# A two-layer encoder on one core: other SBUF places for V's weights, ScalarE function tables loaded at set points, a new instruction order

## The chip, the core and the metric

The kernel runs on one core of one Trainium2 chip. A core has a matrix engine (PE; its weight loads are shown apart as PEld), two vector engines (DVE and POOL), a scalar engine (ACT) and a queue engine (SP) that here only issues DMA transfers. Each engine executes its own instructions strictly in the order in which the program holds them; between engines they wait on semaphores. The metric is the device time of one execution in microseconds, 1428.3 us before the change (median of 3 runs).

## The reference

One sequence of 512 tokens, width 1024, float32, passes through two layers; each has a token mixer and a SwiGLU channel mixer, both with an RMS norm ahead and one behind.

```python
def swiglu(x, w_gate, w_up, w_down):
    return (jax.nn.silu(x @ w_gate) * (x @ w_up)) @ w_down
...
    for layer in range(DEPTH):
        j = layer // N_MIXERS
        h = rms_norm(x, norm_mix_pre[layer])
        if layer % N_MIXERS == 0:
            h = neighbourhood_attention(h, na_w_qkv[j], na_w_o[j], na_rpb[j])
        else:
            h = dilated_attention(h, dil_w_qkv[j], dil_w_o[j])
        x = x + rms_norm(h, norm_mix_post[layer])
        h = rms_norm(x, norm_ffn_pre[layer])
        x = x + rms_norm(swiglu(h, ffn_w_gate[layer], ffn_w_up[layer], ffn_w_down[layer]), norm_ffn_post[layer])
```

Layer 0's mixer is a windowed attention over an 8 x 64 grid of tokens with a relative bias, 16 heads of 64. Layer 1's mixer is a mixture of three dilated sliding-window attentions, each with its own q, k and v (so nine projections of 1024 x 1024), merged by their softmax denominators. The hidden width of SwiGLU is 2816. The softmaxes need Exp, SwiGLU needs Silu.

## The kernel before

**Products.** Every large product is made of three float32r matmuls: each operand is split into a high part `h` (a copy by ACT, line 456) and a low part `l` (a subtraction by DVE, line 457), and `mm3` (lines 468 to 470) adds h x h, h x l and l x h in one PSUM bank. A matmul names a stationary operand, loaded 128 x 128 by PEld, and a moving operand that is streamed; here the stationary one changes with every matmul. The q/k projections (`pp_n`, `pp_d`), the gate and up projections (`gu`) and the v projections (`vn`, `vd`) are Strassen-Winograd products with seven products in place of eight: classes `Seven` and `Values`. In `Seven` (a "unit") the weights are stationary and the activations are streamed; in `Values` and in `v_quarter` (`vp_n`, `vp_d`), which together make V, the weights are streamed and the activations are stationary. Both kinds take 256 columns at a time. The steps of a unit are p1, p2, d1, s2, s4, s3 and x2b, twelve matmuls each; between them ACT and DVE move partial sums out of the bank (`sink`; line 946 is the subtraction between s3 and x2b in the gate and up projections, line 548 the copy between d1 and s4).

**Places.** Split weights go to four pairs of 4096-byte buffers (`wslot`), and where more are needed to parts of `vbig` and of `rxc`. In the built program `rxa`, `rxb` and `rxc`, which hold the split activations, begin at 128 modulo 512 bytes and the buffers of `wslot` at 448; `vbig` begins at 448 too, and its second half lies 536 columns behind the first, that is 96 bytes further modulo 512. The three pairs of buffers that V uses besides (`vslots`) begin at 224 and 448.

**Functions.** ACT holds the table of one set of functions at a time. Copy and Square are in each; the build puts an ACT_TABLE_LOAD ahead of the first Exp or Silu after the other one: lines 681, 948, 1347 and 948 again.

**Order.** The kernel is first recorded, as a list of some 14,700 instructions. `Order` then builds their dependences, runs a list scheduler 20 times forwards and backwards with the costs of `_cost`, takes the ranks of one of these runs (`FIRST`), changes some ranks by the rows of `TABLE`, and pins the order of each engine (`pin`). So a row of the table or a cost moves instructions on all engines. SP's and POOL's DMA issues are ordered so too.

**Stages, by the first and last start of their matmuls in the trace (us).** V of layer 0 from 9, its q/k projections and attention from 45 to 213, the output projection from 180 to 237, gate and up from 239 to 462, down from 460 to 566; V of layer 1 from 567 to 700, its q/k projections and attention from 689 to 1066, the output projection from 1013 to 1088, gate and up from 1090 to 1314, down from 1308 to 1415. Stages overlap where the order lets work of the next one fill gaps.

## Time and profile before

| | |
|---|---|
| runs | 1426.39, 1428.39, 1428.3 us; median 1428.3 |
| profiled execution, own time | 1425.52 us |
| its span | 1423.7 us |
| PE | 1393.9 us busy (98%), 10714 matmuls |
| PEld | 1302.8 us (92%) |
| DVE | 1186.0 us (83%) |
| ACT | 914.8 us (64%) |
| POOL | 534.9 us (38%) |
| DMA | 253.21 MB, mean 178 GB/s |

A matmul is pipelined: its record lasts about 0.28 us while the next begins about 0.115 us later, so that a busy PE says only that it is never empty. How fast it goes is seen from the starts: from how many matmuls fall into a stretch.

### The profile page before, as it was taken

Reading aid. Unit: us, or ns where it says so; the run is one execution under the profiler, and the core shown is the slowest. Engines: PE = TensorE matmul, PEld = TensorE weight load, DVE = VectorE, ACT = ScalarE, POOL = GpSimd, SP = SyncE. Lnnn points to the kernel's source line nnn. Section 1 sums busy time; section 2 is a strip of 40 time slices with the busy share of each in tenths; the row PEclk is TensorE's granted clock in tenths of the full one; section 3 lists DMA queues with packets and bytes.
Section 4 is the critical chain, followed back from the end, with each engine's and each line's share of the span. In section 5 each row is a group of like instructions: output and inputs, shape, how many; then the busy total and the mean of one; then the engine's idle time right before and its main releaser. Section 6 shows DMA issues by size and latency. Waiting matters only on the chain.

```text
span 1423.7 us, 27815 instructions
## 1 busy us (share of the span) xinstructions
PE 1393.9 (98%) x10714; PEld 1302.8 (92%) x10714; DVE 1186.0 (83%) x1891; ACT 914.8 (64%) x1850; POOL 534.9 (38%) x394
## 2 busy tenths in 40 slices
PE   8999999999999999999999999999999999999997
PEld 8998878999999888999999999998888999999886
DVE  7789868899998889997677788887658989988877
ACT  6488865654555667744477687887766555555664
POOL 3756525634320001666454344343215543430001
PEclk9999999999999999999999999999999999999999
DMA  7357598587334665545332353343776797845662
GB/s 254 125 179 192 163 314 240 202 237 214 119 110 137 221 216 173 173 156 179 134 113 75 113 172 98 99 142 98 252 222 216 219 258 219 255 145 164 207 215 96
DMA packets 86645, 253.21 MB, mean 178 GB/s; under 512 B 19312, under 2 KB 31600, under 8 KB 84464
## 3 DMA queue, kind: packets, MB, share of 16 engines
q1 hardware_dynamic: 77696, 197.69, 41.8%
q0 software_dynamic: 8672, 53.48, 15.0%
q8 instruction: 84, 1.38, 0.4%
q14 instruction: 49, 0.40, 0.1%
q10 hardware_dynamic: 144, 0.26, 0.0%
HBM read 229.24 MB, written 68.29 MB: 209 GB/s over the span
## 4 chain that ended last, share of the span: by engine, by line
PE 81%; DVE 9%; ACT 4%; DMA 2%; issue 2%; POOL 0%; POOLq 0%; DVEq 0%; SPq 0%; ACTq 0%
PE gu L468 8%; PE gu L469 8%; PE gu L470 8%; PE pp_d L468 5%; PE pp_d L469 4%; PE pp_d L470 4%; PE yd_s L469 3%; PE yd_s L468 3%; PE yd_s L470 3%; PE vd L469 2%; PE vd L470 2%; PE vd L468 2%; PE yd_pp L470 2%; PE yd_pp L469 2%; PE yd_pp L468 2%
## 5 line engine op out<-in xcount | busy, mean ns | idle before, releaser
L676 POOL TENSOR_TENSOR rs_yd<-v_yd,consts 128x1 f32<-128x1 f32 x8 | 10.0, 1256 | 251.9 <-DVE v_yd L674 251.9
L468 PE MATMUL gu<-rxa,h_c 128*128 128x256 f32 x352 | 98.6, 280 | 1.4 <-DVE mem L944 1.0
L469 PE MATMUL gu<-rxc,h_a 128*128 128x256 f32 x352 | 98.0, 279 | 1.0 <-DVE rxc L693 1.0
L468 PE MATMUL gu<-rxc,h_a 128*128 128x256 f32 x352 | 97.7, 278 | 0.5 <-ACT rxc L690 0.5
L469 PE MATMUL gu<-rxa,h_b 128*128 128x256 f32 x352 | 97.6, 277 | 0.2 <-DVE rxa L693 0.2
L470 PE MATMUL gu<-rxc,l_a 128*128 128x256 f32 x352 | 97.6, 278 | 0.0
L469 PE MATMUL gu<-rxa,h_c 128*128 128x256 f32 x352 | 97.3, 277 | 0.0
L470 PE MATMUL gu<-rxa,l_c 128*128 128x256 f32 x352 | 97.3, 277 | 0.0
L470 PE MATMUL gu<-rxa,l_b 128*128 128x256 f32 x352 | 97.3, 277 | 0.0
L456 ACT ACTIVATE rxc<-mem 128x512 fp32r<-128x512 f32 (+2 forms) x92 | 57.5, 633 | 61.8 <-PE yd_pp L469 32.9
L468 PE MATMUL gu<-rxa,h_b 128*128 128x256 f32 x352 | 97.1, 277 | 0.0
L457 DVE TENSOR_TENSOR rxc<-mem,rxc 128x512 fp32r<-128x512 f32 (+2 forms) x92 | 66.3, 730 | 18.9 <-ACT rxc L456 18.6
L536 POOL TENSOR_TENSOR r_d<-r_d 128x512 f32<-128x512 f32 x24 | 38.4, 1601 | 108.2 <-DVE l_ad L457 83.3
L536 POOL TENSOR_TENSOR raw<-raw 128x512 f32<-128x512 f32 x24 | 36.3, 1514 | 110.0 <-DVE l_a L457 109.9
L536 POOL TENSOR_TENSOR r_gu<-r_gu 128x512 f32<-128x512 f32 x20 | 29.6, 1480 | 116.8 <-DVE l_a L457 104.6
L468 PEld LDWEIGHTS gu<-rxa,h_c 128*128 128x128 f32 x352 | 66.1, 188 | 3.1 <-DVE mem L944 1.7
L469 PEld LDWEIGHTS gu<-rxc,h_a 128*128 128x128 f32 x352 | 66.1, 188 | 1.4 <-DVE rxc L693 1.4
L1347 ACT ACTIVATE mem<-mem 128x256 f32<-128x256 f32 x128 | 63.8, 504 | 5.3 <-DVE mem L1346 5.2
L468 PEld LDWEIGHTS gu<-rxc,h_a 128*128 128x128 f32 x352 | 66.0, 188 | 1.0 <-ACT rxc L690 1.0
L469 PEld LDWEIGHTS gu<-rxa,h_b 128*128 128x128 f32 x352 | 66.1, 188 | 0.4 <-DVE rxa L693 0.4
L469 PEld LDWEIGHTS gu<-rxa,h_c 128*128 128x128 f32 x352 | 66.1, 188 | 0.1
L468 PEld LDWEIGHTS gu<-rxa,h_b 128*128 128x128 f32 x352 | 66.0, 188 | 0.2 <-ACT rxa L690 0.2
(678 smaller groups left out, 6090.4 us busy)
## 6 DMA issues: line engine op xcount, KB each, us to landing
wsum<-wd POOLq DMA_DIRECT2D x24, 1408.0 KB, 11.9
r_d<-dil_qk SPq DMA_DIRECT2D x48, 512.0 KB, 4.0
raw<-wg SPq DMA_DIRECT2D x24, 512.0 KB, 5.4
raw<-wu SPq DMA_DIRECT2D x24, 512.0 KB, 7.8
wsum<-wsum POOLq DMA_DIRECT2D x8, 1408.0 KB, 7.9
raw<-wsum SPq DMA_DIRECT2D x22, 512.0 KB, 4.3
r_gu<-wg SPq DMA_DIRECT2D x20, 512.0 KB, 4.4
r_gu<-wu SPq DMA_DIRECT2D x20, 512.0 KB, 5.5
```

What stands on the lines that cost most here:

```text
L456: act.activation(h, src, AF.Copy)
L457: dve.tensor_sub(l, src, h.bitcast(F32))
L468: i = pe.matmul(o, s[0], m[0], start=start, stop=False, skip_group_check=True)
L469: pe.matmul(o, s[0], m[1], start=False, stop=False, skip_group_check=True)
L470: pe.matmul(o, s[1], m[0], start=False, stop=stop, skip_group_check=True)
L536: self.added = e[0].tensor_add(q[0], q[0], q[2])
L676: pool.tensor_tensor(r, v, mhalf, op=ALU.pow)
L1347: act.activation(pr[:, f], pr[:, f], AF.Exp, bias=st[:, c:c + 1], scale=-1.0, accum_out=st[:, c + 2:c + 3])
```

## The change

**Places.** The buffers of `wslot` become one tile `wring` with four pairs of places. A call with `at=32` (units, output projection, down) takes columns 32 onward, one with `at=0` (V) columns 0 onward; 32 columns are 128 bytes. In the built program `wring` begins at 320 modulo 512 bytes, so V's weights lie at 320 and those of the units at 448 as before. The extra buffers of V move to 320 too (`rxc[:, 48:]` for `rxc[:, 24:]`), except for one low part that stays in `vmem` at 448. The extra weights of layer 0's units (`w22_ring` in `ao`) move from 480 to 448 modulo 512 bytes.

**Functions.** `preset` adds an ACTIVATE of a single column that uses the new function; dependences place it after all uses of the old function (`curves`) and `then` puts it ahead of all uses of the new one. The table load now stands ahead of this small instruction. There are three of them, and four table loads as before.

**Order.** A few costs and delays of the scheduler get other values, a rule is added for float32 matmuls of different areas of the array, and `FIRST` and `TABLE` are new. Apart from the three ACTIVATEs the numbers of instructions that compute or transfer are equal on each engine; only their order differs.

```diff
@@ -43,7 +43,7 @@
-RATE, LANDING, AHEAD, LATE = 350.0, 2300.0, 1000.0, 3000.0
+RATE, LANDING, AHEAD, LATE = 350.0, 2700.0, 1000.0, 900.0
@@ -78,6 +78,8 @@
 
 def _area(i, e):
 
+    if e == 0 and not i.is_transpose:
+        return 1 + (i.outs[0].bass_ap.ap[0][1] == HD)
     aps = [j.bass_ap for j in list(i.outs)[:1] + list(i.ins)[:1] if getattr(j, "bass_ap", None) is not None]
@@ -98,17 +100,19 @@
-        return 350 if e == 4 else 1150 if adds else 560, 1400 * (e == 3), False, 0, size
+        return 470 if e == 4 else 1150 if adds else 560, 1400 * (e == 3), False, 0, size
...
         if str(srcs[0].dtype).endswith("float32r"):
-            return n * 17 / 38.4 + (2.6 if n < 512 else 0.4), n * 17 / 38.4 + 175, False, 0, 0
+            return n * 17 / 38.4 + (1.5 if n < 512 else 0.2), n * 17 / 38.4 + 175, False, 0, 0
...
     if e == 1:
         f = str(getattr(i, "func", ""))
+        if n == 1 and ("Exp" in f or "Silu" in f):
+            return 1500, 1600, False, 0, 0
@@ -142,56 +146,67 @@
-FIRST, TABLE = 17, (
+FIRST, TABLE = 2, (
-    (0, 5, 1038159, 1064323, 11, -818), (2, 0, 10194, 10301, 0, 15467), (0, 5, 948447, 959157, 1, -54352),
...
+    (0, 5, 957181, 993986, 6, 279), (0, 5, 741028, 748810, 14, 3080), (2, 0, 10189, 10217, 0, -1138),
...
@@ -322,6 +337,8 @@
                 if e == 0:
                     if mode > 2:
                         s = max(s + SWITCH.get((kind, 3), 0), half[mode - 3])
+                        if side != self.area[k]:
+                            s, side = max(s, max(half) + 150), self.area[k]
                         half[mode - 3] = s + later - 200
@@ -388,7 +405,7 @@
-    tags, arenas, extra = {}, [], []
+    tags, arenas, extra, curves = {}, [], [], {AF.Exp: [], AF.Silu: []}
@@ -404,8 +421,9 @@
 
-    vbig = cpool.tile([P, D + 32], F32R, name="vbig")
+    vbig = cpool.tile([P, D + 24], F32R, name="vbig")
     vmem = vbig[:, :D]
+    wring = zpool.tile([P, 8 * D + 32], F32R, name="wring")
@@ -417,6 +435,16 @@
+
+    def preset(new, old):
+
+        i = act.activation(consts[:, 40:41], mhalf, new)
+        extra.extend((j.ins.name, i.ins.name) for j in curves[old])
+        curves[old].clear()
+        return i
+
+    def then(i, new):
+        extra.extend((i.ins.name, j.ins.name) for j in curves[new])
 
@@ -443,7 +471,7 @@
-        return tagged(cpool, [P, n], F32, f"small{n}", name, 16 if n > 1 else 12)
+        return tagged(cpool, [P, n], F32, f"small{n}", name, 16 if n > 1 else 9)
@@ -457,12 +485,15 @@
-    def wslot(name):
-        return tuple(tagged(wpool, [P, D], F32R, f"w{i}", f"{i}_{name}", 4) for i in "hl")
-
-    def units2(srcs, name, hls=(None, None), raw=None):
+    places_ = cycle(range(0, 4 * D, D))
+
+    def wslot(at=32):
+        i = next(places_) + at
+        return wring[:, i:i + D], wring[:, i + 4 * D:i + 5 * D]
+
+    def units2(srcs, name, hls=(None, None), raw=None, at=32):
         raw = load2(srcs, name) if raw is None else raw
-        return [split(*(hls[i] or wslot(f"{name}_{i}")), raw[:, i * D:(i + 1) * D]) for i in range(2)]
@@ -515,7 +546,7 @@
-            self.wa = split(*wslot(f"a{self.name}"), self.raw[:, :D])
+            self.wa = split(*wslot(), self.raw[:, :D])
...
@@ -584,10 +615,10 @@
-            self.prod(self.left, split(*wslot(f"a{self.name}"), self.q[0]), X1A, True)
+            self.prod(self.left, split(*wslot(0), self.q[0]), X1A, True)
-            self.prod(self.right, split(*wslot(f"b{self.name}"), self.q[1]), X1B, True)
+            self.prod(self.right, split(*wslot(0), self.q[1]), X1B, True)
...
@@ -750,7 +781,7 @@
-        u = units2(srcs, name, raw=raw)
+        u = units2(srcs, name, raw=raw, at=0)
@@ -846,7 +877,8 @@
-            act.activation(views[i], views[i], AF.Exp, bias=mn[:, i:i + 1], scale=-1.0, accum_out=sm[:, i:i + 1])
+            curves[AF.Exp].append(act.activation(views[i], views[i], AF.Exp, bias=mn[:, i:i + 1], scale=-1.0,
+                                                 accum_out=sm[:, i:i + 1]))
@@ -945,8 +977,8 @@
-                    act.activation(g[:, :256], g[:, :256], AF.Silu)
-                    act.activation(g[:, 256:], left, AF.Silu)
+                    curves[AF.Silu] += [act.activation(g[:, :256], g[:, :256], AF.Silu),
+                                        act.activation(g[:, 256:], left, AF.Silu)]
@@ -1154,9 +1186,11 @@
         hm = mem[:, :FT * 512]
         h2 = hm.rearrange("p (h x) -> p h x", h=2)
         hid = [h2[:, :, f * 256:f * 256 + 256] for f in range(FT)]
+        silu = preset(AF.Silu, AF.Exp)
         with arena(f"raw{layer}", 6 * D) as more:
             gate_up(layer, xs, hid, more, (ring(memc, 0, 512, 5), cycle([memc[:, 2560:3072], mem[:, 13520:14032]]), ring(mem, MEM - 512, 256, 2)),
                     sums[layer])
+            then(silu, AF.Silu)
             def sink(t, xt, hs, gn):
@@ -1201,8 +1235,8 @@
-    ao = inner.enter_context(arena("ao0", 2 * D, "right", F32R))
-    ost_, w22_ = ring(ao, 0, D, 1), w22_ring(ao[:, D:], 512)
+    ao = inner.enter_context(arena("ao0", 2 * D + 40, "right", F32R))
+    ost_, w22_ = ring(ao, 0, D, 1), w22_ring(ao[:, D + 32:], 512)
@@ -1211,7 +1245,7 @@
-                cycle([hl(rxc[:, 24:], 0, D), hl(rxs, 2, D), (vmem, ao[:, :D])]), lambda qd, half, o: None)
+                cycle([hl(rxc[:, 48:], 0, D), hl(rxc[:, 48:], 2, D), (ao[:, :D], vmem)]), lambda qd, half, o: None)
@@ -1264,6 +1298,7 @@
+    exp = preset(AF.Exp, AF.Silu)
     c0 = MEM - 14 * D
     ap = mem[:, c0:]
@@ -1329,7 +1364,7 @@
-        act.activation(d, d, AF.Exp)
+        curves[AF.Exp].append(act.activation(d, d, AF.Exp))
...
@@ -1466,7 +1502,7 @@
-    vus, vslots = {}, cycle([hl(rxc[:, 24:], 0, D), hl(rxs, 2, D), (vmem, rxs[:, 4 * D:])])
+    vus, vslots = {}, cycle([hl(rxc[:, 48:], 0, D), hl(rxc[:, 48:], 2, D), (rxc[:, 48 + 4 * D:48 + 5 * D], vmem)])
@@ -1535,6 +1571,7 @@
                 nc.sync.dma_start(xt[32 * r:32 * r + 16], rows[r, 112:128])
                 nc.sync.dma_start(xt[32 * r + 16:32 * r + 32], rows[r, 0:16])
+    then(exp, AF.Exp)
     inner.close()
     with arena("wm1", 3 * D + 88, "right", F32R) as wm:
         mix_out(1, a["dil_o"], rxb, wm, load_block)
```

Three places of the pinned order, before and after:

SP issues the first transfers in this order before; `x_cols` are the four blocks of tokens, `na_v` the weights of V, two transfers for each quarter of its columns:

```order
L1189 DMA mem<-x_cols 128x1024
L666 DMA mem<-g_mix_pre 128x1024
L452 DMA r_n_126<-na_v 128x1024
L1189 DMA mem<-x_cols 128x1024
L1194 DMA mem<-x_cols 128x1024
L452 DMA r_n_126<-na_v 128x1024
L1194 DMA mem<-x_cols 128x1024
```

and in this one after:

```order
L1223 DMA mem<-x_cols 128x1024
L697 DMA mem<-g_mix_pre 128x1024
L1223 DMA mem<-x_cols 128x1024
L1228 DMA mem<-x_cols 128x1024
L480 DMA r_n_127<-na_v 128x1024
L1228 DMA mem<-x_cols 128x1024
L480 DMA r_n_127<-na_v 128x1024
```

The first weights of V have moved from third to fifth, behind two more blocks of tokens.

ACT at the first use of Silu, at the start of layer 0's gate and up projections (`tr_o` are transposed activations, `gu` units, line 948 the Silu), before:

```order
L690 ACTIVATE rxa<-tr_o_2_6_2763 128x4x128
L940 ACTIVATE memc_2834<-gu_2_2911 128x256
L690 ACTIVATE rxa<-tr_o_2_2_2770 128x4x128
L948 ACT_TABLE_LOAD
L948 ACTIVATE memc_2834<-memc_2834 128x256 x2
L456 ACTIVATE h_b_1_3082<-r_gu_1_2874 128x1024
```

and the load of Silu's table after, some 40 rows earlier (`ta` is the last transposed probability of the attention, `r_wo` the weights of the output projection, `yo` its result):

```order
L896 ACTIVATE mem<-ta_15_2338 128x64
L484 ACTIVATE wm_2366<-r_wo_0_2383 128x1024 x2
L484 ACTIVATE rxb_123<-r_wo_0_2390 128x1024
L1169 ACTIVATE rxa<-o_7_2350 128x512
L441 ACT_TABLE_LOAD
L441 ACTIVATE consts<-consts 128x1
L484 ACTIVATE rxb_123<-r_wo_0_2397 128x1024 x2
```

The load has moved from between two uses of the transposes to the start of the output projection. The other two stand at the start of layer 0's down projection and behind the last Exp of layer 1's mixer, ahead of the weighting of its last heads.

PE at the last scores of layer 1 (`sb` scores with contractions over 64 rows, `o` attention outputs written to 64 partitions, `t` transposes, `yo` the output projection), before:

```order
L1383 MATMUL sb_0_1_11802<-mem 128x128 x2
L1383 MATMUL sb_1_1_11803<-mem 128x128
L1383 MATMUL sb_0_1_11802<-mem 128x128 x2
L1383 MATMUL sb_1_1_11803<-mem 128x128
L1452 MATMUL o_6_11839<-mem 64x256
L1383 MATMUL sb_1_1_11803<-mem 128x128
L1443 MATMUL t_6_11760<-ident,mem 128x128 x4
```

and after:

```order
L1419 MATMUL sb_0_1_11331<-mem 128x128
L1419 MATMUL sb_1_1_11332<-mem 128x128
L1419 MATMUL sb_0_1_11331<-mem 128x128
L1419 MATMUL sb_1_1_11332<-mem 128x128 x2
L1419 MATMUL sb_0_1_11331<-mem 128x128 x2
L1419 MATMUL sb_1_1_11332<-mem 128x128
L1479 MATMUL t_6_11283<-ident,mem 128x128
```

The single `o` no longer stands between the scores.

More of the change, by code (lines that the diff above doesn't have):

```diff
@@ L297, in run @@
         free, locked, half, kind, pipe, now, done = [0.0] * 5, [0.0] * 5, [0.0] * 2, 0, 0.0, 0.0, 0
-        last = [0] * 5
+        last, side = [0] * 5, 0
         heaps, order, wake = [[[] for _ in range(5)] for _ in ENGINES], [[] for _ in ENGINES], []
@@ L458, in split @@
         return h, l
-    def wslot(name):
-        return tuple(tagged(wpool, [P, D], F32R, f"w{i}", f"{i}_{name}", 4) for i in "hl")
-    def units2(srcs, name, hls=(None, None), raw=None):
+    places_ = cycle(range(0, 4 * D, D))
[3 more added lines that the diff above has]
+    def units2(srcs, name, hls=(None, None), raw=None, at=32):
         raw = load2(srcs, name) if raw is None else raw
-        return [split(*(hls[i] or wslot(f"{name}_{i}")), raw[:, i * D:(i + 1) * D]) for i in range(2)]
+        return [split(*(hls[i] or wslot(at)), raw[:, i * D:(i + 1) * D]) for i in range(2)]
     def mm3(o, s, m, start, stop):
@@ L528, in pair @@
         def pair(self, t, src):
-            hl = wslot(f"{t}{self.name}")
+            hl = wslot()
             split(*(v.rearrange("p (i c) -> p i c", c=512) for v in hl), src)
@@ L604, in sums2 @@
             pool.tensor_add(q[1], q[3], q[1])
-            self.w3 = split(*wslot(f"c{self.name}"), q[2])
-            self.w4 = split(*wslot(f"d{self.name}"), q[1])
+            self.w3 = split(*wslot(0), q[2])
+            self.w4 = split(*wslot(0), q[1])
         def d1(self):
@@ L1011, in operands2 @@
         def operands2(x, w, name):
-            h, u = next(hl_), wslot(name)
+            h, u = next(hl_), wslot()
             nx, nw = x.shape[1], w.shape[1]
@@ L1346, in softmax_pair @@
             dve.tensor_tensor_reduce(o, v, bts[i], -1.0, BIG, ALU.add, ALU.min, st[:, c:c + 1])
-            act.activation(pr[:, f], pr[:, f], AF.Exp, bias=st[:, c:c + 1], scale=-1.0, accum_out=st[:, c + 2:c + 3])
+            curves[AF.Exp].append(act.activation(pr[:, f], pr[:, f], AF.Exp, bias=st[:, c:c + 1], scale=-1.0,
+                                                 accum_out=st[:, c + 2:c + 3]))
     def bias(j, hd, k, n):
```

107 rows, old and new, of the table c are left out of this document.

## The prediction

> **What bounds the kernel now.** First the page's busy times and its chain of waits, for the engine that sets the end; then a table by stretches, for where that engine is empty.
>
> ```profile
> PE 1393.9 (98%) x10714; PEld 1302.8 (92%) x10714; DVE 1186.0 (83%) x1891; ACT 914.8 (64%) x1850; POOL 534.9 (38%) x394
> ...
> PE 81%; DVE 9%; ACT 4%; DMA 2%; issue 2%; POOL 0%; POOLq 0%; DVEq 0%; SPq 0%; ACTq 0%
> ```
>
> ```profile
> 0.00:20.00 20.00, 16.19 (x97) 15.08 (x98) 11.40 (x18) 14.35 (x24) 4.94 (x14) 0.91 0.79 283
> 20.00:100.00 80.00, 78.23 (x651) 76.17 (x650) 68.45 (x109) 50.74 (x97) 51.80 (x36) 1.00 0.45 157
> 100.00:1300.00 1200.00, 1183.91 (x9417) 1114.37 (x9416) 1008.63 (x1637) 778.91 (x1622) 472.59 (x341) 1.00 0.58 178
> 1300.00:1423.70 123.70, 115.59 (x557) 97.22 (x555) 97.51 (x131) 70.79 (x111) 5.61 (x4) 0.98 0.53 170
> ```
>
> The first number after the stretch's length is PE's busy time: PE has work everywhere. Between 100 and 1300 us it is empty for 1200 - 1183.9 = 16.1 us; the 3.8 us at the start and the 8.1 us at the end lie outside of it. So the time can fall in two ways: PE's matmuls follow each other faster, or PE is empty or switching less. The clock column is 1.00, so the clock is no third.
>
> How fast they follow is read from PE's count in stretches without a wait: first V of layer 1, then gate and up of layer 1, twice.
>
> ```profile
> 605.00:645.00 40.00, 40.00 (x341) 1.00 0.54 181
> ...
> 1118.00:1158.00 40.00, 40.00 (x353) 1.00 0.93 248
> 1247.00:1296.00 49.00, 49.00 (x432) 1.00 0.48 147
> ```
>
> A record lasts about 0.28 us, so each stretch counts some 2.4 records that began before it: the spacing is 40/338.6 = 118.1 ns in V and 40/350.6 = 114.1, 49/429.6 = 114.1 ns in gate and up, for the same 128x256 matmuls. V is 4.0 ns slower on each.
>
> **The change, part by part.** *Places.* The groups of gate and up between 1118 and 1179 us show what a place does:
>
> ```profile
> L469 PE MATMUL gu<-rxa,h_b 128*128 128x256 f32 x49 | 13.5, 276 | 0.0
> ...
> L469 PE MATMUL gu<-rxa,vbig 128*128 128x256 f32 x12 | 3.4, 285 | 0.0
> L470 PE MATMUL gu<-rxa,vbig 128*128 128x256 f32 x12 | 3.3, 279 | 0.0
> L468 PE MATMUL gu<-rxa,vbig 128*128 128x256 f32 x12 | 3.3, 277 | 0.0
> ```
>
> While line 469 streams, PEld loads the next weights, those of line 470, the low part. In `vbig` it lies 96 bytes further modulo 512 than the high part, and just this matmul takes 285 in place of 276 ns; the other two are near to the usual. So streaming and loading hinder each other by how their places stand. Units stream from 128 and load from 448, a distance of 192 modulo 512. V streams from 448 (or 224) and loads from 128: 320 (or 96). After the change V streams from 320: 192, as the units. V has four quarters of 96 and six units of 168 matmuls, 1392 together; 48 that stream `vmem` keep their distance. The other 1344 x 4.0 ns = **-5.4 us**. Lower end: nothing, if V is slow for another reason (its streamed operand is the weights). Upper end by these two rows of PE's timeline, the fastest spacing of a unit, 10 matmuls in 1.13 us:
>
> ```profile
> 1118.36 0.28 PE L468 MATMUL gu<-rxa,h_c 128*128 128x256 f32 x1
> ...
> 1119.49 0.28 PE L469 MATMUL gu<-rxa,h_c 128*128 128x256 f32 x1
> ```
>
> 1344 x (118.1 - 113.0) = -6.9 us. I take -5.4, the mean over a stretch as long as V.
>
> [...]
>
> *Order, float32 matmuls.* Scores and attention outputs (`sb`, `o`) use half of the array. Here are many `o` together, and one between scores, as in the third place shown ahead:
>
> ```profile
> 818.14 1.95 PE L1452 MATMUL o<-mem 128*64 128x256 f32 x20
> ...
> 1028.01 0.65 PE L1452 MATMUL o<-mem 128*64 128x256 f32 x2
> 1028.59 0.48 PE L1383 MATMUL sb<-mem 64*128 64x128 f32 x2
> ```
>
> Together they cost 1.95/20 = 0.10 us a record; alone the two of one instruction hold PE from 1028.01 to 1028.59, 0.58 us in place of 0.20. So a boundary costs (0.58 - 0.20)/2 = 0.19 us. Counted in both orders, boundaries between `sb`-like and `o`-like matmuls fall from 21 to 5, but more of the rest stand beside other matmuls: all boundaries of float32 matmuls fall from 117 to 105. 12 x 0.19 = **-2.3 us**; between 0, if the dearer kinds are among the new ones, and 16 x 0.19 = -3.0.
>
> *Function tables.* The load ahead of layer 1's first Silu, on ACT:
>
> ```profile
> 1098.27 0.60 ACT L690 ACTIVATE rxa<-tr_o 128x512 fp32r<-128x512 f32 x1
> 1098.88 1.28 ACT L948 ACT_TABLE_LOAD   x1
> 1100.18 0.42 ACT L948 ACTIVATE memc<-memc 128x256 f32<-128x256 f32 x1
> ```
>
> It costs 1.30 us, from 1098.88 to 1100.18, and holds up the next copy of a transpose. What PE paid behind the two Silu loads (252 to 262 and 1098 to 1108 us):
>
> ```profile
> PE gu L469 <- DVE rxa L693: 0.2, 1, 0.2
> ...
> PE tr_o L699 <- DVE rxa L693: 0.8, 2, 0.5
> ```
>
> At most 1.0 us; one of the latter two stands behind a long DVE split instead, so I take 0.5. The load of Exp had no wait of PE behind it. The new places are covered by the output projections, whose matmuls need no ACT for several us, except that the third stands in front of the weighting of the last heads: uncovered, it would cost 1.30 plus the small ACTIVATE, by its nearest row (128x256, 0.42) at most 0.4. Covered, I charge 0.1. Sum **-0.4 us**, from -1.0 to +1.5.
>
> [...]
>
> *Order, the start.* SP now issues two blocks of tokens ahead of V's first weights.
>
> ```profile
> GB/s 0 0 0 98 197 172 328 418 344 319 279 328 401 426 434 410 426 401 426 434 401 401 377 418 442 401 410 410 270 57 8 25 172 262 377 213 82 82 238 426
> ```
>
> ```profile
> 7.72 1.06 ACT L456 ACTIVATE h_n<-r_n 128x1024 fp32r<-128x1024 f32 x1 [2.05 <-DMA r_n<-na_v]
> ...
> 8.81 1.22 DVE L457 TENSOR_TENSOR l_n<-r_n,h_n 128x1024 fp32r<-128x1024 f32 x1 [0.91 <-ACT h_n L456]
> ...
> 11.56 0.39 PE L470 MATMUL vp_n<-h_n,rxa 128*128 128x256 f32 x1 [1.09 <-DVE rxa L693]
> ```
>
> The queue moves about 410 GB/s (slices of 0.5 us), 1.28 us for 512 KB. The first weights land at 7.7 us; two transfers later is 10.3. ACT then finishes the transposes' copies that now stand ahead (to about 11.7), splits (1.06), DVE subtracts (1.22): PE has both parts at about 14.0, where it ran from 11.56. Against these 2.4 us stand the eight transposes that PE has done by then, 0.9, and part of the next wait. I take **+1.0 us**, between 0 and +2.4.
>
> *Order, the rest.* Every stage has a new order, and the work is the same. What it is worth lies in single waits like the longest one now:
>
> ```profile
> 1192.67 3.25 DVE L538 TENSOR_TENSOR r_gu<-r_gu 128x512 f32<-128x512 f32 x1
> ...
> 1198.35 0.39 PE L468 MATMUL gu<-rxa,rxc 128*128 128x256 f32 x1 [2.06 <-ACT mem L548]
> ```
>
> A DVE addition took 3.25 us, ACT's split waited for it, and behind that the copy of line 548 which PE needed. Such meetings of engines are not seen in an order. The tail has the same instructions in the same order behind the last matmul. I take **0**, bounded by half of the 16.1 us as a gain and, as a loss, by the third rival.
>
> Sum: -5.4 - 2.3 - 0.4 + 1.0 = -7.1 us. The profiled execution has 1425.5 us (span 1423.7 and 1.8 around it), so 1418.4 by its own measure. The median of the runs, 1428.3, is 2.8 above it; from there the forecast is **1421.2 us**.
>
> **The rivals.**
>
> *The new order also empties half of PE's idle time.* For it: waits like the 2.06 us above are few and long. Against: they arise from meetings that a new order makes elsewhere. -7.1 - 8.0: 1413 us.
>
> [...]
>
> *The rest of the order gives the gain back* by three more waits of about 2 us: 1427.
>
> *Gate and up becomes late at one point, and the kernel slower.* Between s3 and x2b DVE has to subtract (line 946) before PE can go on.
>
> ```profile
> L946 DVE TENSOR_TENSOR memc<-mem,gu x22: 406/412/422, 269.6 to 1303.1; 128x256 f32<-128x256 f32 x22
> ```
>
> ```profile
> L457 DVE TENSOR_TENSOR l_b<-raw,h_b 128x1024 fp32r<-128x1024 f32 x12 | 15.8, 1313 | 3.1 <-ACT h_b L456 3.0
> ```
>
> In layer 1, PE had 10 or more matmuls to do meanwhile in 21 of 22 units; now ten units have 7 to 9, 0.9 us by 114 ns, and three units of layer 0 no more. If a split (1.31) starts just before s3 ends, the result comes at 1.31 + 0.41 = 1.72 and PE waits 0.8 us and about 0.3 to be released: 13 x 1.1 = 14.3, together +7.2, 1435.5 us. It decides from 0.55 us per such unit. Against: a split stands directly ahead of the subtraction in 15 of 44 units, before in 17.
>
> **How the numbers follow.** Forecast 0.50 (1416.5 to 1425.4), better order 0.17, places without effect 0.10, gain given back 0.12, slower 0.11. Two medians of this kernel are told apart from 0.2%, 2.9 us: faster takes the first two and a part of the fourth, 0.70; within takes the rest of it and the third, 0.19; slower 0.11. The range runs from just below the better order to just above the median before, 1411.5 to 1429: what it leaves out is the slower case and the far end of the second. The likeliest case's own range is 1416.5 to 1425.4.
>
> **What would show it.** V of layer 1: 40 us should hold about 353 matmuls, not 341, and V's records be near 276 ns. If V stays at 118 ns, the first step is wrong. The single `o` between scores should be gone at the end of layer 1's mixer, and PE's busy time with it fall by some 7 us. Behind the two first Silu no wait on line 693's successor should be named. The first V matmuls should run without a break from about 14 us; earlier, and the start was costed too high. PE idle between 100 and 1300 us should stay near 16 us: clearly less is the first rival, clearly more the third, and if waits before x2b in gate and up make it, the fourth.

## The result, and the profile after

The changed kernel takes 1439.33 us (median of 6 runs, 1436.51 to 1443.63) where the kernel before took 1429.13 us in the same series: 1.0071 times as long, 95% interval 1.005 to 1.0091. The forecast was 1421.2 us, faster. The profiled execution has 1437.08 us of its own, with a span of 1435.3 us, 11.6 us more than before.

First the page of the kernel after, its busy times and its chain of waits; then the same stretches that were shown of before.

```profile
PE 1393.2 (97%) x10714; PEld 1301.9 (91%) x10714; DVE 1190.4 (83%) x1891; ACT 913.8 (64%) x1853; POOL 532.0 (37%) x394
...
PE 77%; DVE 12%; ACT 4%; issue 3%; DMA 2%; POOL 1%; POOLq 0%; DVEq 0%; SPq 0%; ACTq 0%
```

```profile
0.00:20.00 20.00, 13.80 (x78) 12.82 (x79) 10.57 (x17) 13.76 (x23) 4.93 (x14) 0.83 0.79 271
20.00:100.00 80.00, 75.66 (x636) 74.08 (x635) 65.24 (x98) 48.24 (x89) 48.21 (x33) 1.00 0.46 157
100.00:1300.00 1200.00, 1176.61 (x9353) 1106.59 (x9352) 1005.98 (x1630) 774.08 (x1621) 474.99 (x344) 1.00 0.57 176
1300.00:1435.30 135.30, 127.11 (x654) 108.44 (x652) 108.61 (x150) 77.71 (x123) 3.88 (x4) 0.99 0.55 177
```

PE is busy as long as before (1393.2 and 1393.9 us), and empty for 42.1 us in place of 29.8: 6.2 us in place of 3.8 in the first stretch, 4.3 in place of 1.8 in the second, 23.4 in place of 16.1 in the third, and 8.2 in place of 8.1 at the end. These 12.3 us, less 0.7 us of busy time, are the slowdown of 11.6. The busy time hides what got faster, because a short wait lies under the record of the matmul ahead of it: from 365.42 to 366.05 us PE of the kernel before starts no matmul for 0.63 us, and is empty for 0.34 of them. So the table takes each matmul from its start to the start of the next one, and the pauses of PE over 0.9 us apart (worked out from all matmuls of the two traces):

| us | before | after |
|---|---|---|
| V, four kinds | 169.3 | 164.7 |
| scores, attention outputs and their transposes (`s`, `sa`, `sb`, `o`, `t`) | 134.7 | 129.2 |
| output projections | 92.5 | 90.2 |
| q/k units of layer 0 | 85.0 | 82.0 |
| q/k units of layer 1 | 245.9 | 251.0 |
| gate and up | 432.8 | 440.9 |
| pauses of PE over 0.9 us | 7.3 (5) | 20.6 (15) |
| the rest | 246.6 | 246.8 |

The first four rows gained 15.4 us, more than was forecast: V 4.6 (forecast 5.4), scores and outputs 5.5 (2.3 for a part of them). The units of layer 1, gate and up, and the pauses took back 26.5 us.

The clock took a part of this. The trace of the change has three stretches at a granted clock of 0.50, from 11.31 us for 6.83, from 280.96 and from 1096.75 for 3.41 each; that of before has one, from 12.69 for 3.41 (those behind the last matmul of each are left out). In the second of them the 128x256 matmuls start 213 ns apart (12 from 281.28 to 283.84 us), and 118 ns apart behind it (44 from 284.44 to 289.62): 45% of the time is the clock's there. Taken for all matmuls that start in these stretches, the long pauses left out, this is 5.2 us in place of 1.6. By this estimate, worked out from these starts, the clock makes some 3.7 of the 11.6 us, 2.9 of them in gate and up.

Six of the 15 pauses, by PE's timeline (in brackets the idle time and what ended it):

```profile
11.56 0.47 PE L730 MATMUL tr_a<-ident,mem 128*128 128x128 f32 x1 [2.53 <-DVE v_a L703]
...
14.86 0.58 PE L500 MATMUL vp_n<-wring,rxa 128*128 128x256 f32 x1 [1.00 <-DVE wring L485]
...
279.54 0.38 PE L499 MATMUL gu<-rxc,wring 128*128 128x256 f32 x1 [2.15 <-ACT wring L484]
...
939.98 0.39 PE L499 MATMUL pp_d<-rxb,rxc 128*128 128x256 f32 x1 [1.69 <-ACT memc L579]
...
1097.10 0.58 PE L500 MATMUL gu<-rxc,wring 128*128 128x256 f32 x1 [1.42 <-DVE rxc L724]
...
1215.20 0.39 PE L499 MATMUL gu<-rxc,wring 128*128 128x256 f32 x1 [1.19 <-ACT wring L484]
```

Several steps end them; the splits into `wring` (lines 484 and 485) recur. So there are three suspects: the new order, the shared tile `wring`, and V's new places.

### The profile page after: what moved, and what is told of

Its sections match the earlier page's. It is cut to its first block, busy times and chain, and to the rows that moved or that the text cites. A ratio compares the mean times of both kernels' runs of the same rounds, so it can differ in the third digit from the quotient of the medians.

```text
span 1435.3 us, 27816 instructions
## 1 busy us (share of the span) xinstructions
PE 1393.2 (97%) x10714; PEld 1301.9 (91%) x10714; DVE 1190.4 (83%) x1891; ACT 913.8 (64%) x1853; POOL 532.0 (37%) x394
## 4 chain that ended last, share of the span: by engine, by line
PE 77%; DVE 12%; ACT 4%; issue 3%; DMA 2%; POOL 1%; POOLq 0%; DVEq 0%; SPq 0%; ACTq 0%
PE gu L499 8%; PE gu L501 8%; PE gu L500 8%; PE pp_d L499 5%; DVE wring L485 4%; PE pp_d L501 4%; PE pp_d L500 4%; PE yd_s L499 3%; PE yd_s L500 3%; PE yd_s L501 3%; PE yd_pp L500 2%; PE yd_pp L499 2%; PE yd_pp L501 2%; PE yo L501 2%; PE yo L499 2%
## 5 line engine op out<-in xcount | busy, mean ns | idle before, releaser
L499 PE MATMUL gu<-rxa,wring 128*128 128x256 f32 x704 | 193.6, 281 | 1.5 <-DVE mem L978 1.3
L501 PE MATMUL gu<-rxa,wring 128*128 128x256 f32 x704 | 190.4, 278 | 2.2 <-DVE wring L485 2.2
L500 PE MATMUL gu<-rxa,wring 128*128 128x256 f32 x704 | 192.3, 277 | 0.0
L485 DVE TENSOR_TENSOR wring<-r_d,wring 128x1024 fp32r<-128x1024 f32 x112 | 142.9, 1283 | 39.9 <-ACT wring L484 39.2
L485 DVE TENSOR_TENSOR wring<-raw,wring 128x1024 fp32r<-128x1024 f32 (+1 forms) x120 | 156.0, 1302 | 16.8 <-ACT wring L484 16.2
L484 ACT ACTIVATE wring<-raw 128x1024 fp32r<-128x1024 f32 x120 | 122.4, 1020 | 61.2 <-PE gu L500 31.2
L484 ACT ACTIVATE wring<-r_d 128x1024 fp32r<-128x1024 f32 x112 | 115.8, 1040 | 33.2 <-PE gu L500 9.5
L499 PEld LDWEIGHTS gu<-rxa,wring 128*128 128x128 f32 x704 | 131.3, 188 | 4.5 <-DVE mem L978 2.3
L501 PEld LDWEIGHTS gu<-rxa,wring 128*128 128x128 f32 x704 | 130.3, 188 | 3.3 <-DVE wring L485 3.2
L500 PEld LDWEIGHTS gu<-rxa,wring 128*128 128x128 f32 x704 | 131.9, 188 | 0.2
L499 PE MATMUL pp_d<-rxa,wring 128*128 128x256 f32 x384 | 108.2, 284 | 2.4 <-ACT wring L484 0.9
L500 PE MATMUL pp_d<-rxa,wring 128*128 128x256 f32 x384 | 106.6, 280 | 0.0
L501 PE MATMUL pp_d<-rxa,wring 128*128 128x256 f32 x384 | 105.5, 280 | 0.0
L499 PE MATMUL gu<-rxc,wring 128*128 128x256 f32 x352 | 98.5, 282 | 5.2 <-ACT wring L484 3.3
L500 PE MATMUL gu<-rxc,wring 128*128 128x256 f32 x352 | 99.0, 282 | 1.4 <-DVE rxc L724 1.4
L501 PE MATMUL gu<-rxc,wring 128*128 128x256 f32 x352 | 98.7, 282 | 0.4 <-DVE wring L485 0.3
L484 ACT ACTIVATE wring<-r_gu 128x1024 fp32r<-128x1024 f32 x60 | 63.5, 1058 | 50.6 <-PE gu L500 23.5
L485 DVE TENSOR_TENSOR wring<-r_gu,wring 128x1024 fp32r<-128x1024 f32 x60 | 76.9, 1284 | 13.2 <-ACT wring L484 12.9
```

The costliest lines, as they stand in the source:

```text
L484: act.activation(h, src, AF.Copy)
L485: dve.tensor_sub(l, src, h.bitcast(F32))
L499: i = pe.matmul(o, s[0], m[0], start=start, stop=False, skip_group_check=True)
L500: pe.matmul(o, s[0], m[1], start=False, stop=False, skip_group_check=True)
L501: pe.matmul(o, s[1], m[0], start=False, stop=stop, skip_group_check=True)
```

## The experiments

To tell these apart the order must be held while the rest changes. In all runs below the planner is replaced by a list of all instructions: each engine takes them in the list's order, and one that would stand ahead of what it needs goes behind it. The list is that of the kernel before, that of the change, or one up to a time of the planner and the other behind it.

```diff
-    order.pin(tc, 20, FIRST, TABLE)
+    order.pin(tc, PLACES)
```

Each ratio is to the kernel before on the same chip, with its 95% interval.

| run | order | V's place | slots of `wring` | tables early | us | ratio |
|---|---|---|---|---|---|---|
| the change | new | 192 | in turn | yes | 1439.33 | 1.0071 (1.005 to 1.0091) |
| places_only | before | 192 | in turn | no | 1451.26 | 1.0154 (1.0137 to 1.017) |
| old_order | before | 192 | in turn | yes | 1446.89 | 1.0123 (1.0101 to 1.0145) |
| old_places | new | 320 | in turn | yes | 1442.16 | 1.009 (1.0069 to 1.011) |
| ring_old_places | before | 320 | in turn | no | 1432.77 | 1.0029 (1.0018 to 1.004) |
| freed_old_places | before | 320 | as before | no | 1427.53 | 1.0001 (0.999 to 1.0013) |
| free_slots | before | 192 | free first | no | 1436.57 | 1.0053 (1.0034 to 1.0073) |
| after_free | new | 192 | free first | yes | 1437.8 | 1.0066 (1.0041 to 1.0091) |
| tables_only | before | 320 | as before | yes | 1426.44 | 0.999 (0.998 to 1.0) |
| calm_slots | before | 192 in part | free first | no | 1427.75 | 0.9997 (0.9985 to 1.0008) |
| calm_all | before | 192 in part | free first | yes | 1429.54 | 1.0008 (0.9995 to 1.0021) |

### Places and order, one without the other

Edits: places_only leaves the three `preset` calls out and takes the order before; old_order keeps the calls; old_places takes the new order with V back at 320 modulo 512.

```diff
-        u = units2(srcs, name, raw=raw, at=0)
+        u = units2(srcs, name, raw=raw)
...
-            self.prod(self.left, split(*wslot(0), self.q[0]), X1A, True)
+            self.prod(self.left, split(*wslot(), self.q[0]), X1A, True)
```

> The changed kernel without its three small ACTIVATEs, every engine's order that of the kernel before (its one difference: about 20 instructions around 40 to 55 us, where the weights of V and of the query and key units now share 32 columns of one tile). Theory A (the places are worth what the spacing says, the new order loses it): 1429.1 - 5.4 = 1423.7 us. Theory B (one shared tile for all weights, or the new places, cost more than they bring; the order is innocent): 1429 or more. If places are worth nothing to V: 1429.

> The changed kernel with its three small ACTIVATEs and its places, every engine's order that of the kernel before, the ACTIVATEs behind the same neighbours as in the change. Against the kernel above it shows the function tables alone. Theory A: 1423.7 - 0.4 = 1423.3. Theory C (the early tables hold ACT up and make PE wait): 1.5 to 5 us above the kernel above, 1425 to 1429.

> The changed kernel, its order kept instruction for instruction, with all weights of V back at a distance of 320 modulo 512 from the tokens. Theory A: the gain of the places falls away, 1439.3 + 5.4 = 1444.7. Theory B: at most 1439.

> The changed kernel with the order of the kernel before for all that the planner starts in the first 105 us, its own order behind that. Theory A with the start as one of its losses: PE's idle time in the first 100 us was 5.0 us more than before and falls away, 1439.3 - 5.0 = 1434.3. If the start's idle time is made up for later, or the order before does not fit the later one: 1438 to 1440.

The last one takes the order before for the first 105 us and the new one behind it: 1452.47 us, ratio 1.0166 (1.015 to 1.0181). Theory A, the gain of the places eaten by the order, falls with the first run: with its order unchanged the kernel is 22 us slower. Undoing the places in the new order costs 2.8 us, half of the 5.4, and the two intervals overlap. start_old mixes the order before with V at 192 and slots in turn, as places_only does. In its trace the last matmul of the first output projection starts at 253.8 us, where it is 245.8 in places_only and 238.5 in the change: PE waits 7.7 us for two splits into the ring, and the granted clock is 0.91 from 20 to 105 us and 0.93 from there to 240. So it says nothing of the start by itself.

### The slots

In the kernel before the four pairs of buffers are tiles of a pool, and a split takes one that is free. With `wring` a call takes the next of four in turn, and a weight of V in columns 0 to 1023 of its slot shares 32 columns with a unit's weight in the slot beside it (columns 32 to 1055 of that). The edit of the next runs is a list of slots, one for each of the 348 calls:

```diff
-        i = next(places_) + at
-        return wring[:, i:i + D], wring[:, i + 4 * D:i + 5 * D]
+        h, l = (x * D + at for x in divmod(int(next(slots_), 16), 4))
+        return wring[:, h:h + D], wring[:, l + 4 * D:l + 5 * D]
```

> The kernel of the run places_only with all weights of V back at 320 modulo 512: the order before, no small ACTIVATEs, the places before, and of the change only that the weights take the four slots of one tile in a fixed turn. Theory D (the fixed turn makes a split wait for a slot that PE is still reading, where before it got the slot that came free first): 1451.3 + 5.4 = 1456.7, or somewhat less, as the 32 columns that slots of V and of units share go too; at least 1445. Theory E (the 32 shared columns are the loss, the turn is innocent): 1429.

> The kernel above with one thing more undone: each weight takes the same slot that it had in the kernel before (a list of 348 slots in place of the turn). Order, places and slots are then those of the kernel before. Theory D: 1429, as before. If one tile in place of eight, or the order written down as a list, costs by itself: as the kernel above.

> The kernel of the run places_only (the order before, V at 192 modulo 512, no small ACTIVATEs), each weight in the slot whose last reader on PE comes first in the order, the 32 shared columns counted. Theory A and D together: 1429 - 5.4 = 1423.7, and 0 to 3 for the waits on shared columns that remain where V and units meet: 1423 to 1427. If V's places are worth nothing: 1429 to 1432.

> The changed kernel, its order kept instruction for instruction, only that each weight takes the slot whose last reader on PE comes first in place of the next in turn: 44 of ACT's waits and 34 of DVE's are for an earlier instruction. Theory D: most of the 12.3 us of idle time that PE gained goes, 1427 to 1433. If the new order itself is the loss: 1437 to 1440.

freed_old_places is the kernel before again, 1.0001: neither the list nor the single tile costs anything that can be told. The fixed turn costs 0.28%, 4.0 us; its 1432.77 us lie below what theory D asked for (1445 or more) and above theory E (1429). It is seen in ACT's waits, where line 576, or 584 in the second kernel, is the split and gu stands for PE's matmuls of gate and up (total us, times, longest). First ring_old_places:

```profile
ACT wring L576 <- PE gu L593: 25.7, 29, 2.9
ACT wring L576 <- PE gu L592: 15.4, 10, 3.7
```

and freed_old_places:

```profile
ACT wring L584 <- PE gu L601: 21.0, 22, 3.0
ACT wring L584 <- PE gu L600: 6.3, 5, 2.3
```

41.1 us of waits of the split in place of 27.3, in the same order. In the change itself one row of them has 64.2 us:

```profile
ACT wring L484 <- PE gu L500: 64.2, 36, 4.9
```

free_slots gets the turn out of the way and keeps V at 192, and is still 0.52% slower than freed_old_places, 7.4 us: there the shared columns are left. Its PE waits for splits into the ring, just where V and units meet:

```profile
PE pp_n L599 <- ACT wring L584: 2.0, 1, 2.0
...
PE pp_d L599 <- ACT wring L584: 1.8, 1, 1.8
...
PE pp_d L601 <- DVE wring L585: 1.5, 2, 0.8
...
PE pp_n L601 <- DVE wring L585: 0.8, 1, 0.8
```

These are 6.1 us, and calm_slots below, which keeps V at 320 where the two meet, has none of them and is 0.56% quicker, 8.0 us. Turn and shared columns do not simply add up. places_only, with both, is 1.53% slower than freed_old_places, 21.9 us, where 4.0 and 7.4 make 11.4: with V at 192 the turn costs 14.4 us (places_only against free_slots). Part of that is the clock: behind the first 20 us the trace of places_only has four stretches of 3.41 us at a granted clock of 0.50, those of free_slots and freed_old_places one each; by the 213 ns in place of 118 above a stretch costs some 1.5 us, an estimate. The rest was not followed further.

The new order was planned with both. There, slots that are free first gain 0.05%, which the intervals do not tell from nothing; by the expectation this speaks for the order itself as the loss. What the turn and the shared columns cost within the new order stays open.

### Tables, and V's places without their side effects

> Order, slots and places of the kernel before, and only the three small ACTIVATEs of the change, each behind the neighbour it has in the change. As forecast: 1427.5 - 0.4 = 1427.1. Theory C (ACT is held up where PE needs it): 1429 to 1431. If they are the gain of 4.4 us that the runs old_order and places_only seem to show: 1423.

> The order and the wait structure of the kernel before (the slot for each weight from a list), no small ACTIVATEs; V at 192 modulo 512 only where its weights do not meet those of units in the shared tile: V's quarters and units of layer 1, and the weights that lie outside of that tile, 997 of PE's pairs of matmuls in place of none. Theory A (4.0 ns each, and nothing else): 1427.5 - 997 x 0.0040 = 1423.5. If V's places are worth nothing by themselves: 1427.5.

> The kernel of the run calm_slots with the three small ACTIVATEs, and with the one stretch of V's units that was still at 320 modulo 512 (24 matmuls of each unit, whose low part lay in vbig) at 192 too for the units 1 to 4: its low part lies in columns that are free until the query and key units begin. One DMA of the bias goes 15 places later on SP's queue. In calm_slots the spacing in V was 113.5 ns until such a stretch at 630 us by the profile and 117.8 ns from there to the end of V, with the same places before and behind it. Theory G (there are two steady spacings at 192, and a stretch at 320 can push the matmuls behind it into the slow one): without those stretches V stays at 113.5 ns, 969 x 4.2 ns = 4.1 us, and the tables' 1 us: 1428.1 - 5.1 = 1423. Theory H (the slow spacing comes by itself, whatever the places): 117.8 ns over much of V, 1426.5 to 1427.

The tables gain 1.4 us, between 0 and 2.9, as forecast or a little more; the 4.4 us between places_only and old_order, whose intervals overlap, did not come back. calm_slots holds V at 192 only where its weights meet no unit's:

```diff
-        h, l = (x * D + at for x in divmod(int(next(slots_), 16), 4))
+        n, s = next(slots_)
+        at = 0 if 142 <= n < 164 else 32
+        h, l = (x * D + at for x in divmod(int(s, 16), 4))
```

and calm_all brings the last stretch of four V units to 192 as well:

```diff
-    vus, vslots = {}, cycle([hl(rxc[:, 48:], 0, D), hl(rxc[:, 48:], 2, D), (rxc[:, 48 + 4 * D:48 + 5 * D], vmem)])
+    vus, vslots = {}, iter([v for x in (low,) * 4 + (vmem,) for v in (
+        hl(rxc[:, 48:], 0, D), hl(rxc[:, 48:], 2, D), (rxc[:, 48 + 4 * D:48 + 5 * D], x))])
```

Neither gains: theory A's 4 us are not there, and theory G falls with calm_all, where V goes over to the slow spacing with no stretch at 320 near it. Theory H is nearest in V, though not in time (1429.54 for 1426.5 to 1427). Two windows of calm_all, both in V of layer 1 and both at 192 (length, then PE's busy time and count):

```profile
586.00:601.00 15.00, 15.00 (x134) 14.91 (x133) 14.90 (x12) 11.18 (x16) 11.60 (x5) 1.00 0.38 125
635.00:675.00 40.00, 40.00 (x342) 40.00 (x341) 32.23 (x22) 18.94 (x24) 26.70 (x10) 1.00 0.53 180
```

With 2.4 records taken off as in the prediction, the spacing is 15/131.6 = 114.0 ns in the first and 40/339.6 = 117.8 ns in the second. Between them stands a short wait of PE:

```profile
602.90 0.36 PE L601 MATMUL vd<-rxc,rxb 128*128 128x256 f32 x1
603.42 0.39 PE L601 MATMUL vd<-rxc,rxb 128*128 128x256 f32 x1 [0.17 <-ACT p5b L743]
603.65 0.29 PE L602 MATMUL vd<-rxc,rxb 128*128 128x256 f32 x1
```

Ahead of it each matmul begins 113 or 114 ns behind the last; behind it 117 or 118, for 84 us, until the first q/k unit. In the change V kept the quick spacing. Its window, with 40/349.6 = 114.4 ns:

```profile
635.00:675.00 40.00, 40.00 (x352) 39.98 (x351) 37.24 (x23) 19.07 (x24) 25.34 (x9) 1.00 0.54 178
```

So there are two steady spacings. How many of V's matmuls, among others of V and not held up, are quick (115.5 ns or less), counted in the traces:

| V at | kernels | share of quick ones |
|---|---|---|
| 320 | before and the seven with all of V there | 0.01 to 0.11 |
| 192 | the change | 0.72 |
| 192 | the ten others, where V is there | 0.25 to 0.82 |
| 320 | calm_slots, calm_all (V of layer 0 and the last unit) | 0.16, 0.41 |

In these kernels a place shifted the odds and did not decide: every kernel with all of V at 320 lies below every one with V at 192, but in calm_all the matmuls at 320 were quick more often than those at 192. What decides was not found. There the spacing changed over at a wait of 0.17 us; in the change V passed one of 0.41 us at 621.12 and was back at 113 or 114 ns from 622.59 on.

The change has one more sign that a place acts. In each unit of V one step, s2, still streams a low part at 448, in `vmem` (`vbig` in the rows). Four rows of the change, the first of them ahead of such a step, the second its first record from `vbig`, the third and fourth behind it:

```profile
632.86 0.28 PE L500 MATMUL vd<-rxc,rxb 128*128 128x256 f32 x1
...
635.58 0.28 PE L500 MATMUL vd<-vbig,rxb 128*128 128x256 f32 x1
...
638.29 0.28 PE L500 MATMUL vd<-wring,rxa 128*128 128x256 f32 x1
...
641.01 0.28 PE L500 MATMUL vd<-wring,rxb 128*128 128x256 f32 x1
```

Between them lie 24, 23 and 24 matmuls without a wait: 2.72/24 = 113.3 ns, 2.71/23 = 117.8 ns, and 2.72/24 = 113.3 ns again. The same is seen in the next two of these steps, from 649.00 and from 674.04 us: 2.71/23 = 117.8 ns in each, 113 or 114 ns ahead of it and behind. No run tells the place from the step: calm_all moves this part to 192, but its V was slow before the first such step came.

### Where the new order loses

Three kernels take the new order up to a time of the planner and the order before behind it, all with V at 320, slots in turn and tables early; old_places is the whole new order.

> The changed kernel with V at 320 (run old_places, 1442.2), the change's order for what the planner starts in the first 240 us (start and layer 1's attention stage), the order before behind that. By the last output projection's matmul, which came 1.4 us later with the new order than with the old one in the profiled executions (250.0 and 248.6): 1432.8 + 1.4 = 1434.2. If most of the order's 9.4 us arises there: 1440.

> The same with the change's order up to 570 us (attention, gate-up and down of the first layer), the order before behind that. By the first matmul of the next layer's V, 584.1 with the new order and 577.9 with the old: 1432.8 + 6.2 = 1439.0. If the first gate-up is not where the order loses: 1434 to 1435.

> V at 320; the change's order up to 1030 us (both attention stages, the first layer's gate, up and down), the order before behind that. It stands between new_to_570 with 1439.9 and the whole new order with 1442.2. Theory F (pauses all along the way: of those over 0.9 us, 3 between 570 and 1030, 4 in the last gate and up): 1441 to 1442. If the new order is only bad in the first layer: 1439 to 1440; if it is better in the second attention stage by itself: 1436 to 1438.

"Layer 1's attention stage" in the first should read the first layer's. Measured were 1435.99, 1439.92 and 1438.96 us:

| new order up to | ratio | interval |
|---|---|---|
| none (ring_old_places, tables late) | 1.0029 | 1.0018 to 1.004 |
| 240 us | 1.0054 | 1.004 to 1.0068 |
| 570 us | 1.0089 | 1.0072 to 1.0107 |
| 1030 us | 1.0085 | 1.0071 to 1.0099 |
| all (old_places) | 1.009 | 1.0069 to 1.011 |

Up to 240 us the new order brings a loss of 0.25%, 3.6 us (5.0, if the tables' 1.4 are added), though these two intervals touch; up to 570 us another 0.35%, 5.0 us. Behind that no difference on the whole can be told. Where the time goes is seen from the profiled executions, one for each kernel, cut at the first matmuls of gate and up and of V of layer 1 (us):

| kernel | up to gate and up | gate, up, down | V and attention of layer 1 | its gate, up, down |
|---|---|---|---|---|
| before | 239.1 | 327.8 | 522.9 | 333.9 |
| freed_old_places | 241.1 | 328.3 | 524.1 | 334.0 |
| ring_old_places | 240.0 | 327.6 | 525.4 | 337.8 |
| new_to_240 | 241.5 | 328.6 | 525.9 | 338.9 |
| new_to_570 | 241.6 | 333.7 | 525.9 | 337.4 |
| new_to_1030 | 241.9 | 333.6 | 524.7 | 337.3 |
| old_places | 241.9 | 331.9 | 524.0 | 345.7 |
| the change | 240.7 | 333.1 | 520.7 | 340.9 |

Against ring_old_places the new order loses 4 to 6 us in gate, up and down of the first layer. Up to there it loses 1 to 2 us, no more than before and freed_old_places lie apart, which have the same order; so, as far as one execution of each tells, the 3.6 us are not all spent there. The second layer is not free of loss: its gate, up and down take 3 to 8 us more with the new order, and V and attention ahead of them give back 1 to 5 (the 5 in the change, with V at 192). Of the 11.6 us between the executions of before and the change, 7.0 stand in the last gate, up and down, 3.9 of which the turn brings with the order before too.

One pause of the first gate and up could be followed to its cause. POOL issues two transfers one behind the other, and just behind them SP issues the weights that PE needs next; these are the rows of the change, of POOL and SP, and then of DMA with the median time to landing:

```profile
265.08 1.16 POOL L1010 DMA_DIRECT2D wsum<-wsum  x2
```

```profile
268.11 3.10 SPq L480 DMA_DIRECT2D r_gu<-wg  x2
271.26 0.43 SPq L480 DMA_DIRECT2D r_gu<-wu  x1
```

```profile
wsum<-wsum POOLq DMA_DIRECT2D x2, 1408.0 KB, 9.9
...
r_gu<-wg SPq DMA_DIRECT2D x2, 512.0 KB, 10.6
r_gu<-wu SPq DMA_DIRECT2D x1, 512.0 KB, 15.7
```

The 512 KB take 10.6 us to land. ACT's split of them waits for that, and PE, whose row stands above, waits 2.15 us for the split, until 279.54:

```profile
278.43 1.06 ACT L484 ACTIVATE wring<-r_gu 128x1024 fp32r<-128x1024 f32 x1 [3.33 <-DMA r_gu<-wg]
```

Three last runs mend this pause, those of the start, and both together with slots that are free first. The edit for the first is in the order of the transfers:

```diff
-POOL: wsum<-wsum, wsum<-wsum, wsum<-wd, r_gu, r_gu, raw, raw
+POOL: wsum<-wsum, r_gu, wsum<-wsum, r_gu, raw, wsum<-wd, raw
-SP: r_gu<-wg (unit 5), r_gu<-wg (unit 6), r_gu<-wu (unit 5)
+SP: r_gu<-wg (unit 5), r_gu<-wu (unit 5), r_gu<-wg (unit 6)
```

> The changed kernel, its order kept but for three DMAs in the first layer's gate and up: GpSimd's second addition of down-weights and the one behind it are issued behind the additions of the next units' weights that they stood in front of, as before the change, and the second half of unit 5's gate weights directly behind the first. Theory F (single meetings in the new order: here two transfers of 1408 KB stand just ahead of 512 KB that PE needs next): PE's pause of 2.15 us at 279.5 goes, and with it the clock of 0.50 of the 3 us behind it, 1.5 us: 1439.3 - 3.7 = 1435.6. If the weights are late for another reason: 1439.

> The changed kernel with the order of the kernel before for what the planner starts in the first 30 us, its own order behind that. Theory F: the three pauses of PE there, 1.44 + 2.53 + 1.00, become the one of 1.09 of the kernel before: 1439.3 - 3.9 = 1435.4. If the time is made up for by the stage behind it, as the end of the output projection only 1.4 us later suggests: 1438 to 1440.

> Both of these edits, and each weight in the slot whose last reader comes first in the order (1.5 us in the run after_free). Theory F, if the parts add up: 1439.3 - 3.7 - 3.9 - 1.5 = 1430.2. If each mended pause only lets another one grow: 1435 or more.

Measured were 1438.51 us (1.0081, 1.0067 to 1.0096), 1437.4 us (1.0073, 1.0054 to 1.0091) and 1434.75 us (1.0052, 1.0037 to 1.0068). In no_clash the weights land in time,

```profile
r_gu<-wg SPq DMA_DIRECT2D x2, 512.0 KB, 5.6
r_gu<-wu SPq DMA_DIRECT2D x1, 512.0 KB, 6.7
```

the pause is gone, and from the last output projection to the first matmul of the next V its profiled execution takes 332.9 us in place of 335.3; but the whole does not get shorter. In the two traces V takes 2.1 us more, as V of layer 1 runs at 117 to 118 ns for most of its length, and attention takes 1.8 more. In start_30 the output projection ends 1.7 us earlier, and the whole is the same. All three edits together bring 0.19%, 2.7 us of the 9.1 expected, and their interval overlaps that of the change. So single pauses can be mended, but of what they are worth less than a third is seen at the end, and even that is not told from nothing. No version was found that beats the kernel before by more than the measurement tells; the nearest is tables_only.

## Why the prediction was wrong

**The sum.** Along one path of runs the parts add up to 10.0 of the 10.2 us: the fixed turn +4.0 (ring_old_places against freed_old_places), the new order with the early tables +8.7 (old_places against that), V's places with the shared columns -2.7 (the change against that). By another path they differ: with the order before, V's places with the shared columns cost 17.9 us (places_only against ring_old_places).

**Places, -5.4.** As a saving it came nearly true in the change: V takes 4.6 us less, and the sign for it came, 352 matmuls in 40 us where 353 were forecast. What failed is the step from a place to a spacing, "streaming and loading hinder each other by how their places stand". One matmul of 285 beside 276 ns was taken for the cause of a spacing that has two steady values at either place; with the order before, the gain did not arrive at all (calm_slots, calm_all). That places have no effect and V is slow for another reason, which was given 0.10, is right about calm_slots (0.9997) and not about the change, where V did become quick. The shares, 0.01 to 0.11 against 0.25 to 0.82, speak against it, and the quick matmuls at 320 in calm_all (0.41) speak for it; no run here settles it.

**What no term held.** The prediction priced where V's weights lie and not how a slot is given out. One tile in place of eight buffers brought two waits, the fixed turn (4.0 us in the order before) and the 32 shared columns (7.4 to 8.0 us there); both together cost 21.9. Both could be read in the diff: `wslot` counts through four places, and `at` moves V's slot onto its neighbour.

**Order, float32 matmuls, -2.3.** Right in sign and too small. The groups of `sb` and of one kind of `o`, first of before, then of after (busy time, mean ns):

```profile
L1383 PE MATMUL sb<-mem 64*128 64x128 f32 x256 | 26.1, 295 | 0.0
...
L1452 PE MATMUL o<-mem 128*64 128x256 f32 (+1 forms) x160 | 20.3, 346 | 0.0
```

```profile
L1419 PE MATMUL sb<-mem 64*128 64x128 f32 x256 | 21.8, 292 | 0.0
...
L1488 PE MATMUL o<-mem 128*64 128x256 f32 (+1 forms) x160 | 17.8, 344 | 0.0
```

By their starts all `sb` and `o` together take 70.8 us in place of 74.9, so -4.1. No run takes the boundaries alone. The sign named for the whole, PE's busy time lower by some 7 us, did not come: it fell by 0.7, since waits hide in it.

**Function tables, -0.4.** -1.4 in tables_only, with zero at the edge of its interval. The sign to look for, no wait of PE on the split of transposes at the start of gate and up, did not come: the row of 1097.10 above is just such a wait, with no table load near it. That wait belongs to the order.

**Order, the start, +1.0.** The pauses over 0.9 us of the first 20 us grew from 1.1 to 5.0, and the first product of V came at 13.3 us, as forecast (14). The step failed in taking the wait ahead of V for the only one: the transposes of the second block of tokens wait too, 2.53 us at 11.56. What it is worth at the end is not settled, as start_30 shows no gain.

**Order, the rest, 0.** This is the step that failed in size. With places and slots alike, the new order costs 0.61%, 8.7 us (1.0090 against 1.0029; 10 with the tables' gain added), in place of 0. By the traces it arises in gate, up and down of both layers, and V and attention of the second give some back. Why it arises there was followed for one pause only; the rest of the cause stays open. The sentence that such meetings "are not seen in an order" was right, and the conclusion from it wrong: it made the most uncertain term a zero in the middle of the range, with 0.11 for all that lies above it.

**The rivals.** The fourth, gate and up late at one point, forecast 1435.5 us by waits of units for the subtraction ahead of x2b. The time is near the measured one by luck, as the waits that came are others. No row of the runs shows its 0.3 us to be released: the subtraction that ends at 365.99 us in the kernel before releases the matmul at 366.05, 0.06 us later. PE's waits in the kernel after (total us, times, longest), of which only the last of these rows is that subtraction:

```profile
PE gu L499 <- ACT wring L484: 3.3, 2, 2.2
PE tr_a L730 <- DVE v_a L703: 2.5, 1, 2.5
PE gu L501 <- DVE wring L485: 2.5, 5, 0.9
PE gu L499 <- ACT rxc L721: 1.9, 2, 0.9
...
PE gu L499 <- DVE mem L978: 1.3, 2, 1.1
```

PE's idle time between 100 and 1300 us, the sign for rivals three and four, did point the right way: 23.4 us in place of 16. The third rival, the gain given back, had the right kind of loss, more pauses, and too few of them: ten more over 0.9 us with 13.3 us together, in place of three of about 2.

## What to carry to other kernels

When buffers of a pool become slots of one tile, price how slots are given out, and which of them overlap, before the gain of the move. When a change brings a new order of everything, a run of each order with all else held is worth more than any reading of its parts; until then its term needs a range as wide as the kernel's idle time on both sides. A gain of a few ns on each matmul should be looked for in the whole stretch of the changed kernel, not taken from one pair of rows.

## What the runs showed of the hardware

**Two steady spacings.** In these traces chains of 128x256 float32r matmuls at the same places ran at 113.5 ns or at 117.8 ns each, at the full granted clock, and kept that for up to 84 us, in V as in shorter stretches of units (in gate and up of the kernel before, 56 in a row at 117.8 ns from 1239.7 us). The prediction read the slow one as a property of V.

**One pause cost twice.** Behind the pause of 2.15 us the granted clock (third column from the end) falls to 0.50 for 3.41 us. The 16 matmuls that start there stand 213 ns apart in place of 118, some 1.5 us more; these are windows of the change:

```profile
279.00:280.00 1.00, 0.46 (x3) 0.46 (x4) 0.48 (x1) 1.00 (x3) 0.00 (x0) 1.00 0.97 237
280.00:281.00 1.00, 0.90 (x7) 0.68 (x6) 1.00 (x2) 0.98 (x2) 0.00 (x0) 0.98 1.08 270
281.00:282.00 1.00, 1.00 (x6) 1.00 (x6) 1.00 (x3) 0.29 (x1) 0.00 (x0) 0.50 1.00 253
282.00:283.00 1.00, 1.00 (x7) 1.00 (x7) 0.95 (x2) 0.13 (x1) 0.00 (x0) 0.50 1.07 266
283.00:284.00 1.00, 1.00 (x6) 1.00 (x6) 0.72 (x2) 0.13 (x1) 0.00 (x0) 0.50 1.05 260
284.00:285.00 1.00, 1.00 (x9) 1.00 (x8) 0.20 (x1) 0.77 (x2) 0.00 (x0) 0.81 1.03 250
```

In no_clash, without this pause, the clock stays at 1.00 there:

```profile
281.00:284.00 3.00, 2.98 (x26) 2.78 (x25) 2.95 (x5) 1.35 (x3) 1.52 (x1) 1.00 0.97 347
```

It came behind some pauses only: behind the 2.06 us at 1198.35 in the kernel before, the clock stayed at 1.00. In no_clash it fell to 0.50 for 3.4 us behind a pause of 1.74 us at 940.13, and in the change it did not behind one of 1.69 us at 939.98.
